# Delta rule: where the third substitution and the second and third merges stand

## The chip, the core and the metric

One core of a Trainium2 chip runs the whole program in one launch. The metric is the device time of that launch in microseconds, as the median of several runs. The text names the engines as the profile does: PE (TensorE: matrix products, transposes; PEld is its weight load), DVE (VectorE), ACT (ScalarE), POOL (GpSimd) and SP (SyncE, which only issues transfers). Each works through its own queue in order; they wait for each other through semaphores. POOL and ACT issue transfers too.

## What is computed

Two layers of a mixer and a mixture of experts, over 256 context and 512 latent tokens. In the mixer, eight heads of softmax attention and eight heads of a gated delta rule, run in both directions, share one input and one output projection. The change concerns the delta rule alone. For each chunk of 64 tokens and each head it needs the inverse of a unit lower triangle, `tmat`:

```python
lower = jnp.where(strict, jnp.einsum("bhnid,bhnjd->bhnij", kb, kc) * decay, 0.0)
tmat = lax.linalg.triangular_solve(lower + eye, jnp.broadcast_to(eye, lower.shape),
                                   left_side=True, lower=True, unit_diagonal=True)
u = jnp.einsum("bhnij,bhnje->bhnie", tmat, vc * bc)
w = jnp.einsum("bhnij,bhnjd->bhnid", tmat, kb * jnp.exp(gcum)[..., None])
...
def step(state, xs):
    v_new = u_i - jnp.einsum("bhid,bhde->bhie", w_i, state)
    o_i = jnp.einsum("bhid,bhde->bhie", qd_i, state) + jnp.einsum("bhij,bhje->bhie", a_i, v_new)
    state = state * jnp.exp(gl_i)[..., None, None] + jnp.einsum("bhid,bhie->bhde", kd_i, v_new)
    return state, o_i
```

The scan over the chunks is serial; there are 12 chunks, context first, and the second direction runs backwards through the context's and then the latents' chunks.

## The kernel before, in words

Tokens stand in six tiles of 128 (two of context, four of latents), two chunks in a tile. A layer goes through these stages: normalization; projections with convolutions, in which the triangles are also built and inverted; the attention's loop, in which attention and the serial delta steps are interleaved; output projection and routing; experts.

*Triangles.* They are worked on in three batches of two tiles, `PAIRS = ((0, 1), (2, 5), (3, 4))`. For a batch, `intra_batch` builds the triangles (`delta_intra`): the two 32 x 32 diagonal blocks of each go to memory (`db`), the block off the diagonal stays in SBUF (`uo`). `delta_subst` inverts the diagonal blocks: it loads the batch as `sB`, one 32 x 32 triangle per partition, and runs 31 pairs of DVE operations, a product into `sT` (L821) and a subtraction from `sY` (L822), each pair on the result of the one before. The result goes to memory (`dy`, L823). `delta_merge` loads it in another layout (`yl`, L834), transposes it on DVE (`yt`, L835), multiplies the blocks on PE (L848, L852, in the PSUM tile `mg`), adds the parts up in `xm` (ACT L840, DVE L856) and stores the inverses to memory (`xad`, L857).

*Where these stand.* The string `ORDER` gives the order of the projection stage, by layer. "c" is a convolution's projection, "n" a plain one, "i", "s" and "m" are `intra_batch`, `delta_subst` and `delta_merge` with the number of the batch. All three substitutions and all three merges stand in it; the third merge is its last item.

*The attention's loop.* For each of the 12 delta steps a pattern (`PAT`) is read letter by letter: "f" advances attention by a quarter of a block of 128 queries and one head, "d" advances the delta step by one part, "a" computes a quarter of a modulation chunk from a 1 MB load (`araw`, issued by POOL) and adds it to `ac` (L264, L266, L279, stored at L280). A delta step reads `xad`, `vk` and `qkd` of its two tiles, loaded one step ahead by SP (`step_load`, L867 to L873). Steps 0 to 3 read the tiles of the first batch, 4 and 5 those of the second, 6 and 7 those of the third. Before the loop, `kv_stacks` loads `vl` and `xl` (POOL, L558, L563) and builds the attention's keys and values; `attn_queries` turns the queries (L586).

*PSUM.* Eight banks are three tiles of tag "a", three of tag "c" and one of tag "s", which is two banks wide. Attention's scores (L601, `sc`) take "s", and so does the merge's `mg`. For each block of queries: scores on PE, row maxima on DVE (L605), exp on ACT (L610), scale, turn, split, values.

*Order.* The program is given to a planner that places the instructions of each engine by the program's order and by its own estimate of when they are ready. `pin` fixes an order by hand where `pins(True)` is set; in the loop it is off (L1619).

## Time and profile before

| | us |
|---|---|
| median of three runs | 2127.5 (2121.08 to 2129.52) |
| the profiled execution, its time | 2123.24 |
| the profiled execution, its span | 2121.4 |
| PE busy in the span | 1758.6 (83%) |
| DVE busy | 1272.5 (60%) |
| ACT busy | 882.0 (42%) |
| POOL busy | 839.4 (40%) |

The profile is of one execution; times in it count from the first instruction. "Busy" is the time in which an engine ran an instruction, and a share of the span is a mean over stages with different limits; hence the views by stretch below. A row of a timeline gives start, duration, engine, line of the kernel, operation, tiles (out<-in), and in brackets how long the engine had been idle and what released it.

### The profile page before, as it was taken

The numbers are of one execution on the slowest core, as the hardware profiler recorded it, in microseconds if no ns is written. First come the engines' busy times: TensorE is split into PE (matmuls) and PEld (weight loads), VectorE is DVE, ScalarE is ACT, GpSimd is POOL, SyncE is SP. The second block draws the span as 40 slices with busy tenths as digits, with TensorE's granted clock in tenths as the row PEclk, the third lists the DMA queues.
The fourth block names the chain that finished last, engine by engine and source line by source line (L and its number), as shares of the span: only waits on it lengthen the run. The fifth ranks groups of instructions, "written<-read, shape, count | busy, mean of one in ns | idle before, by whom it ended". The sixth has DMA issues, their size and how long they took to land. (4 is left out here: it accounts for less than half of the span.)

```text
span 2121.4 us, 34943 instructions
## 1 busy us (share of the span) xinstructions
PE 1758.6 (83%) x13579; PEld 1287.2 (61%) x13579; DVE 1272.5 (60%) x2350; ACT 882.0 (42%) x1513; POOL 839.4 (40%) x915
## 2 busy tenths in 40 slices
PE   6998785678887869999996987844897769999995
PEld 4886775456666745565555876733576555566553
DVE  3468995467672445655555579984677453444443
ACT  3454333446561124444444544423565223444442
POOL 4455663253254323324225467640334632233221
PEclk9998897779997989999997998976999779999997
DMA  8223445986627398889854323365972668887872
GB/s 279 72 70 90 117 137 144 260 250 204 195 56 171 103 359 315 328 319 324 327 180 122 92 73 110 93 182 148 311 204 71 177 266 311 328 312 303 313 262 85
DMA packets 227684, 427.76 MB, mean 202 GB/s; under 512 B 83721, under 2 KB 157181, under 8 KB 202940
## 3 DMA queue, kind: packets, MB, share of 16 engines
q1 hardware_dynamic: 171547, 329.09, 46.1%
q0 software_dynamic: 33536, 72.59, 12.1%
q10 hardware_dynamic: 22432, 23.81, 3.3%
q8 instruction: 109, 1.79, 0.4%
q14 instruction: 60, 0.48, 0.1%
HBM read 386.82 MB, written 84.67 MB: 222 GB/s over the span
## 5 line engine op out<-in xcount | busy, mean ns | idle before, releaser
L1351 PE MATMUL pab<-w,xt 128*128 128x512 f32 x1024 | 465.0, 597 | 0.5 <-ACT xt L1345 0.5
L1351 PEld LDWEIGHTS pab<-w,xt 128*128 128x128 f32 x1024 | 189.3, 192 | 191.2 <-issue 186.3
L1405 POOL DMA_INDIRECT yd<-ey,idx x64 | 118.8, 1856 | 469.8 <-DMA yd<-ey,idx 196.1
L1372 DVE TENSOR_TENSOR gl<-gt,gh 128x256 fp32r<-128x256 f32 x64 | 27.2, 425 | 276.9 <-ACT gh L1371 265.2
L1330 DVE TENSOR_TENSOR w2l<-w,w2h 128x2048 fp32r<-128x2048 f32 x64 | 147.3, 2301 | 43.5 <-ACT w2h L1329 40.8
L1371 ACT ACTIVATE gh<-gt 128x256 fp32r<-128x256 f32 x64 | 24.6, 385 | 349.1 <-PE gt L1367 349.1
L486 POOL TENSOR_TENSOR wlo<-wraw,whi 128x1024 fp32r<-128x1024 f32 (+1 forms) x44 | 111.1, 2530 | 83.5 <-ACT whi L485 83.5
L236 PE MATMUL pn<-whi,hh 128*128 128x256 f32 (+1 forms) x432 | 134.5, 314 | 8.7 <-ACT gev L1541 4.7
L236 PE MATMUL pn<-wlo,hh 128*128 128x256 f32 (+1 forms) x432 | 134.2, 312 | 4.6 <-POOL wlo L486 4.6
L236 PE MATMUL po<-woh,m 128*128 128x512 f32 x320 | 114.4, 434 | 28.1 <-ACT m L1040 15.7
L236 PE MATMUL pn<-whi,hl 128*128 128x256 f32 (+1 forms) x432 | 133.3, 313 | 0.7 <-DVE hl L347 0.6
L236 PE MATMUL pt<-hh,wlo 128*128 128x512 f32 (+1 forms) x352 | 124.8, 354 | 0.0
L236 PE MATMUL pt<-hl,whi 128*128 128x512 f32 (+1 forms) x352 | 123.4, 351 | 0.0
L236 PE MATMUL pt<-hh,whi 128*128 128x512 f32 (+1 forms) x352 | 122.5, 348 | 0.0
L1329 ACT ACTIVATE w2h<-w 128x2048 fp32r<-128x2048 f32 x64 | 121.7, 1902 | 0.0
L1393 PE MATMUL py<-w2h,gh 128*128 128x512 f32 x256 | 108.1, 422 | 4.4 <-DVE ey L1400 4.4
L515 DVE SCALAR_TENSOR_TENSOR dT<-xin,cw,dT 128x772 f32<-128x772 f32 x64 | 82.7, 1295 | 43.9 <-ACT dT L513 42.2
L1345 ACT ACTIVATE xt<-xt 128x512 f32<-128x512 f32 x128 | 69.8, 596 | 85.4 <-PE xt L1344 85.3
L1393 PE MATMUL py<-w2l,gh 128*128 128x512 f32 x256 | 102.1, 399 | 0.0
L1393 PE MATMUL py<-w2h,gl 128*128 128x512 f32 x256 | 101.5, 396 | 0.0
L610 ACT ACTIVATE pp<-sc,mx 128x768 f32<-128x768 f32 (+1 forms) x80 | 65.3, 816 | 83.5 <-DVE mx L605 83.2
L236 PEld LDWEIGHTS pn<-whi,hh 128*128 128x128 f32 x432 | 90.8, 211 | 13.5 <-ACT gev L1541 4.9
(391 smaller groups left out, 4443.9 us busy)
## 6 DMA issues: line engine op xcount, KB each, us to landing
w<-w SPq DMA_DIRECT2D x192, 1024.0 KB, 9.2
araw<-ada_w POOLq DMA_DIRECT2D x40, 1024.0 KB, 9.7
wraw<-w_in SPq DMA_DIRECT2D x40, 512.0 KB, 4.3
lk<-vk SPq DMA_DIRECT2D x48, 256.0 KB, 7.2
lx<-xad SPq DMA_DIRECT2D x40, 256.0 KB, 6.9
araw<-ada_w SPq DMA_DIRECT2D x8, 1024.0 KB, 10.6
wr<-w_out SPq DMA_DIRECT2D x8, 1024.0 KB, 5.1
vk<-vr ACTq DMA_DIRECT2D x16, 384.0 KB
```

The costliest lines, as they stand in the source:

```text
L236: self.nc.tensor.matmul(ps, a(k), b(k), start=(first and n == 0), stop=(last and n == 3 * nk - 1))
L486: getattr(nc, eng).tensor_tensor(lo, raw, hi, op=OP.subtract)
L515: nc.vector.scalar_tensor_tensor(dst, xin[:, tap:tap + 772], cw[:, tap, f:f + 1], dst, op0=OP.mult, op1=OP.add)
L610: self.pin(self.nc.scalar.activation(u.p[:, :u.nk * P], u.ps[:, :u.nk * P], AF.Exp, bias=u.mx, accum_out=u.sm))
L1329: self.pin(nc.scalar.activation(hi, src, AF.Copy))
L1330: self.pin(eng.tensor_tensor(lo, src, hi, op=OP.subtract))
L1345: pin(nc.scalar.activation(xt[:, 4 * q:4 * q + 4, :], ps.rearrange("p (k n) -> p k n", k=4), AF.Copy))
L1351: self.pin(self.nc.tensor.matmul(pa.rearrange("p (a f) -> p a f", a=2), xt[:, k, :], w13[:, :, k, :], start=(k == 0), stop=(k == 7)))
L1371: pin(nc.scalar.activation(gh, p3, AF.Copy))
L1372: pin(nc.vector.tensor_tensor(gl, p3, gh, op=OP.subtract))
L1393: pin(self.nc.tensor.matmul(py[:, n * 512:(n + 1) * 512], a[:, j, :], b[:, c], start=(j + m == 0), stop=(j == 1 and m == 2)))
L1405: self.pin(self.nc.gpsimd.indirect_dma_start(out=yd, out_offset=bass.IndirectOffsetOnAxis(ap=idx, axis=0), in_=y, in_offset=None, bounds_c ...
```

## The change

The third substitution and the second and third merges leave `ORDER` and are done inside the attention's loop, on generators that are advanced between the letters of the pattern: the substitution by one pair of operations per letter in steps 0 and 1, the second merge in step 2 and the third in step 4, each in five parts, before letters 0, 6, 9, 13 and 17. The merge's PSUM tiles are now two of tag "c" in place of one of tag "s". The blocks off the diagonal of the second and third batch go to memory (`ud`) and come back as `ul`. The substitution's triangle and result and the merges' `yl` and `yt` share one buffer there (tag "yl"), `xm` has one. For room, `ac`, `ql` and `lq` go from two buffers to one, `uo` from six to four, and `yt2` shares the buffers of `ot`.

```diff
-UO = 6
+UO = 4
+XM = 1
+MG, MG1, MA = {2: 1, 4: 2}, 2, (0, 6, 9, 13, 17)
...
-ORDER = ("c4 c5 c6 c7 S i0 s0 i1 s1 i2 s2 c0 c1 c2 c3 Q n256 n0 x n512 m0 m1 c8 c10 c11 c9 n2304 m2",
-         "c4 c5 c6 c7 S c0 i0 s0 i1 s1 c9 i2 s2 c1 c2 c3 Q n256 n0 x n512 m0 m1 c8 c10 n2304 c11 m2")
+ORDER = ("c4 c5 c6 c7 S i0 s0 i1 s1 i2 c0 c1 c2 c3 Q n256 n0 x n512 m0 c8 c10 c11 c9 n2304",
+         "c4 c5 c6 c7 S c0 i0 s0 i1 s1 c9 i2 c1 c2 c3 Q n256 n0 x n512 m0 c8 c10 n2304 c11")
...
-        acc = pool.tile([P, UNIT], F32, tag="ac", bufs=2, name="ac")
+        acc = pool.tile([P, UNIT], F32, tag="ac", bufs=1, name="ac")
...
-        x = pool.tile([P, 4, P], F32, tag="ql", bufs=2, name="ql")
+        x = pool.tile([P, 4, P], F32, tag="ql", bufs=1, name="ql")
...
-    def delta_subst(self, b, db, dy, pool):
+    def delta_subst(self, b, db, dy, pool, one=False):
+        nc, pin = self.nc, self.pin
+        if one:
+            both = pool.tile([P, 2 * D], F32, tag="yl", bufs=1, name="sBY")
+            B, Y = [both[:, n * D:(n + 1) * D].rearrange("p (a b) -> p a b", a=32) for n in range(2)]
...
+            pin(nc.vector.tensor_tensor(Y[:, j + 1:32, 0:w], Y[:, j + 1:32, 0:w], T3, op=OP.subtract))
+            yield
         self.q("iy").dma_start(dy.rearrange("h q r c -> (h q) r c"), Y)
+        yield
...
+    def delta_merge(self, tts, dy, us, ud, xad, pool):
+        both = pool.tile([P, 2 * D], F32, tag="yl", bufs=1, name="yl")
+        yl, yt = [both[:, n * D:(n + 1) * D].rearrange("p (d t h i) -> p d t h i", d=2, t=2, h=NH) for n in range(2)]
...
+        if us is None:
+            us = {}
+            for j, tt in enumerate(tts):
+                us[tt] = pool.tile([P, NH, 32], F32, tag="ul%d" % j, bufs=1, name="ul")
+                self.q("ild").dma_start(us[tt], ud[j])
+        yield
+        pin(nc.vector.transpose(yt, yl))
...
-        ps = self.psS("mg")
-        pa, pb = ps[:, :512], ps[:, 512:]
+        pa = self.psC("mga")
...
+        pin(nc.scalar.activation(g, pa, AF.Copy, scale=-1.0))
+        x = []
+        for d in range(2):
+            x.append(pool.tile([P, 2, NH, HD], F32, tag="xm", bufs=XM, name="xm"))
+            for q in range(2):
+                pin(nc.scalar.activation(x[d][:, :, :, 32 * q:32 * q + 32], xb[d], AF.Copy, scale=self.C["quad"][:, q:q + 1]))
+        yield
+        pb = self.psC("mgb")
...
-            a = pool.tile([P, 512], F32, tag="lq", bufs=2, name="lq")
+            a = pool.tile([P, 512], F32, tag="lq", bufs=1, name="lq")
...
-            t = pool.tile([P, 512], F32, tag="yt2", bufs=1, name="yt2")
+            t = pool.tile([P, 512], F32, tag="ot", bufs=2, name="yt2")
...
+        if b > 0:
+            for j, tt in enumerate(PAIRS[b]):
+                self.q("iud").dma_start(ud[b, j], us[tt])
...
-            with self.pool("q2", A) as p2:
+            with self.pool("q2", A) as p2, self.pool("mg2", A) as p3:
                 S, seen = [None], set()
+                subst = self.delta_subst(2, db[2], dy[2], p3, True)
...
-                    for c in PAT[i][s % 3]:
+                    for n, c in enumerate(PAT[i][s % 3]):
+                        if s in MG:
+                            if n == 0:
+                                b = MG[s]
+                                assert next(subst, None) is None
+                                merge = self.delta_merge(PAIRS[b], dy[b], None, ud[b], xad, p3)
+                            if n in MA:
+                                next(merge)
+                        if s < MG1:
+                            next(subst, None)
                         next({"d": step, "f": fill, "a": ada}[c], None)
```

## Rows read from the trace of the kernel before

**Rows 1.** The page: tenths of busy time, VectorE, in 40 slices

```profile
DVE  3468995467672445655555579984677453444443
```

**Rows 2.** Busy time by stretch: stretch, length, busy by engine, PEclk, DMA share, GB/s

```profile
187.00:345.00 158.00, 128.06 (x1498) 115.52 (x1497) 152.66 (x313) 57.05 (x111) 89.78 (x80) 0.89 0.38 111
345.00:378.00 33.00, 5.44 (x265) 4.87 (x265) 7.55 (x16) 8.96 (x17) 8.62 (x10) 0.58 0.71 192
378.00:640.00 262.00, 212.00 (x2807) 157.72 (x2808) 174.15 (x369) 145.19 (x293) 104.99 (x109) 0.89 0.68 197
1301.00:1412.00 111.00, 84.37 (x884) 72.83 (x884) 106.53 (x242) 37.92 (x79) 64.25 (x55) 0.86 0.38 107
1412.00:1471.00 59.00, 14.73 (x547) 11.78 (x548) 29.74 (x60) 17.05 (x28) 10.83 (x11) 0.56 0.60 179
1471.00:1641.00 170.00, 144.92 (x2275) 111.63 (x2273) 124.49 (x258) 101.23 (x189) 57.85 (x64) 0.94 0.69 200
```

**Rows 3.** Timeline of SyncE, layer 0: Y leaves and comes back

```profile
342.94 0.33 SPq L823 DMA_DIRECT2D dy<-sY  x1
345.76 6.26 SPq L834 DMA_DIRECT2D yl<-dy  x4
```

**Rows 4.** Timeline of VectorE, layer 0: the third merge's transpose

```profile
362.34 1.25 DVE L835 STREAM_TRANSPOSE yt<-yl 128x1024 f32<-128x1024 f32 x1 [17.21 <-DMA cr<-conv_w]
```

**Rows 5.** Timeline of TensorE: first scores; last projection and qt, layer 1

```profile
377.88 0.55 PE L601 MATMUL sc<-ka,qs 128*128 128x256 f32 x1 [9.23 <-DVE xm L856]
...
1411.11 0.39 PE L236 MATMUL pt<-hh,wlo 128*128 128x512 f32 x1
...
1424.08 0.42 PE L586 MATMUL qt<-cst,ql 128*128 128x128 f32 x1
...
1469.91 0.76 PE L601 MATMUL sc<-ka,qs 128*128 128x512 f32 x1 [5.39 <-DVE xm L856]
```

**Rows 6.** Sums of L821, of L822, both layers; L821 alone; L821 after 1412

```profile
sum 314.00, DVE 92.35; mean DVE 46.18
...
sum 314.00, DVE 85.70; mean DVE 42.85
...
L821 DVE TENSOR_TENSOR sT<-sB,sY x186: 178/377/2585, 187.1 to 1447.3; 128x31 f32<-128x31 f32 x12, 128x60 f32<-128x60 f32 x12, 128x87 f32<-128x87 f32 x12, 128x112 f32<-128x112 f32 x12
...
1412.00:1450.00 38.00, 7.88 (x18) 0.59 0.73 222
```

**Rows 7.** The merges' pieces: last additions, xm's waits, TensorE in one merge

```profile
L856 DVE SCALAR_TENSOR_TENSOR xm<-mg,cst,xm x12: 737/748/752, 302.4 to 1469.0; 128x512 f32<-128x512 f32 x12
...
  DMA xad<-xm: 25.9, 5
...
363.50:369.00 5.50, 3.21 (x252) 0.66 0.41 136
```

**Rows 8.** Timeline of POOL: the attention's first load, by layer

```profile
344.92 0.95 POOL L558 DMA_DIRECT2D vl<-qd  x1
...
1412.67 1.01 POOL L558 DMA_DIRECT2D vl<-qd  x1 [7.65 <-issue]
```

**Rows 9.** The first 56 us of the loops, columns as in rows 2

```profile
378.00:434.00 56.00, 38.56 (x531) 26.44 (x532) 26.07 (x71) 26.27 (x74) 19.32 (x24) 0.74 0.98 278
...
1471.00:1527.00 56.00, 44.69 (x643) 32.45 (x641) 35.87 (x72) 30.42 (x58) 14.05 (x18) 0.89 0.99 294
```

**Rows 10.** Landing of the ten stores of a modulation chunk (L280)

```profile
DMA to landing us min/median/max: 6.2/8.4/10.7
```

**Rows 11.** Timeline, layer 0: a chunk's last add, the next chunk's first copy

```profile
446.35 0.42 DVE L279 TENSOR_TENSOR ac<-ac,ab 128x256 f32<-128x256 f32 x1
...
450.01 0.38 ACT L264 ACTIVATE ac<-aps 128x256 f32<-128x256 f32 x1
```

**Rows 12.** Timeline, layer 1: a POOL issue beside the substitution

```profile
1440.20 0.74 POOL L228 DMA_DIRECT2D araw<-ada_w  x1 [10.53 <-issue]
...
1440.40 0.38 DVE L821 TENSOR_TENSOR sT<-sB,sY 128x207 f32<-128x207 f32 x1
```

More of the change, by code (lines that the diff above doesn't have):

```diff
@@ L807, in delta_intra @@
         self.q("iud").dma_start(db.rearrange("h q j i -> (q j) h i"), src)
-    def delta_subst(self, b, db, dy, pool):
-        nc = self.nc
-        B = pool.tile([P, 32, 32], F32, tag="sB", bufs=SB, name="sB")
+    def delta_subst(self, b, db, dy, pool, one=False):
[3 more added lines that the diff above has]
+            B, Y = [both[:, n * D:(n + 1) * D].rearrange("p (a b) -> p a b", a=32) for n in range(2)]
+        else:
+            B = pool.tile([P, 32, 32], F32, tag="sB", bufs=SB, name="sB")
+            Y = pool.tile([P, 32, 32], F32, tag="sY", bufs=YB, name="sY")
         self.q("ild").dma_start(B, db.rearrange("h q j i -> (h q) j i"))
-        Y = pool.tile([P, 32, 32], F32, tag="sY", bufs=YB, name="sY")
         nc.gpsimd.memset(Y, 0.0)
@@ L834, in delta_merge @@
                 self.q("ild").dma_start(yl[:, d, t], dy[:, n:n + 4].rearrange("h q r c -> (q r) h c"))
-        nc.vector.transpose(yt, yl)
+        if us is None:
[5 more added lines that the diff above has]
+        pin(nc.vector.transpose(yt, yl))
         xb, xt = (yt[:, 0], yl[:, 1]), (yl[:, 0], yt[:, 1])
-        x = [pool.tile([P, 2, NH, HD], F32, tag="xm", bufs=1, name="xm") for d in range(2)]
-        for d in range(2):
-            for q in range(2):
-                nc.scalar.activation(x[d][:, :, :, 32 * q:32 * q + 32], xb[d], AF.Copy, scale=self.C["quad"][:, q:q + 1])
+        yield
         g = pool.tile([P, 512], F32, tag="mg", bufs=1, name="mg")
-        ps = self.psS("mg")
-        pa, pb = ps[:, :512], ps[:, 512:]
+        pa = self.psC("mga")
         place = [(d, 32 * (2 * c2 + d), 32 * (2 * c2 + 1 - d)) for d in range(2) for c2 in range(2)]
@@ L847, in delta_merge @@
             for d, ra, rb in place:
-                nc.tensor.matmul(pa[rb:rb + 32, c], us[tts[t]][ra:ra + 32, h, :], xt[d][ra:ra + 32, t, h, :], start=True, stop=True, tile_position=(ra, rb))
-        nc.scalar.activation(g, pa, AF.Copy, scale=-1.0)
+                pin(nc.tensor.matmul(pa[rb:rb + 32, c], us[tts[t]][ra:ra + 32, h, :], xt[d][ra:ra + 32, t, h, :], start=True, stop=True, tile_position=(ra, rb)))
+        pin(nc.scalar.activation(g, pa, AF.Copy, scale=-1.0))
[4 more added lines that the diff above has]
+                pin(nc.scalar.activation(x[d][:, :, :, 32 * q:32 * q + 32], xb[d], AF.Copy, scale=self.C["quad"][:, q:q + 1]))
+        yield
+        pb = self.psC("mgb")
         for t, h, c in blocks:
             for d, ra, rb in place:
-                nc.tensor.matmul(pb[ra:ra + 32, c], g[rb:rb + 32, c], xb[d][rb:rb + 32, t, h, :], start=True, stop=True, tile_position=(rb, ra))
+                pin(nc.tensor.matmul(pb[ra:ra + 32, c], g[rb:rb + 32, c], xb[d][rb:rb + 32, t, h, :], start=True, stop=True, tile_position=(rb, ra)))
+        yield
         a, b = tts
@@ L855, in delta_merge @@
             y = x[d][:, :, :, 32 - 32 * d:64 - 32 * d]
-            nc.vector.scalar_tensor_tensor(y, pb.rearrange("p (t h i) -> p t h i", t=2, h=NH), self.C["quad"][:, d:d + 1], y, op0=OP.mult, op1=OP.add)
+            pin(nc.vector.scalar_tensor_tensor(y, pb.rearrange("p (t h i) -> p t h i", t=2, h=NH), self.C["quad"][:, d:d + 1], y, op0=OP.mult, op1=OP.add))
             self.q("ix").dma_start(xad[a:b + 1:b - a, d, :, 0].rearrange("t p f -> p t f"), x[d].rearrange("p t h i -> p t (h i)"))
+        yield
     def step_load(self, s, vk, xad, qkd, need, pool):
@@ L994, in token_rows, with intra_batch @@
         self.q("vk").dma_start(dst.rearrange("t p f -> p t f"), r.rearrange("p t e i -> p t (e i)"))
-    def intra_batch(self, b, us, dT, sc, xad, db, pool):
+    def intra_batch(self, b, us, ud, dT, sc, xad, db, pool):
         kk = [self.delta_kk(tt, 1, dT, pool) for tt in PAIRS[b]]
@@ L1591, in layer @@
                         elif kind == "i":
-                            self.intra_batch(int(arg), us, dT, sc, xad, db[int(arg)], p1)
+                            self.intra_batch(int(arg), us, ud, dT, sc, xad, db[int(arg)], p1)
                         elif kind == "s":
-                            self.delta_subst(int(arg), db[int(arg)], dy[int(arg)], p1)
+                            for _ in self.delta_subst(int(arg), db[int(arg)], dy[int(arg)], p1):
+                                pass
                         elif kind == "m":
-                            self.delta_merge(PAIRS[int(arg)], dy[int(arg)], us, xad, p1)
+                            for _ in self.delta_merge(PAIRS[int(arg)], dy[int(arg)], us, None, xad, p1):
+                                pass
                         elif kind == "x":
```

9 lines of the change are left out of this document (3 added, 6 removed).

## The prediction

> **What bounds the kernel now.** I read the page's slices first: VectorE is at 5 to 7 tenths in the projection and delta stages of both layers and at 3 to 5 in the experts [rows 1]. The change touches only the former, so the next view is the busy time by stretch [rows 2]. Six stretches matter, three in each layer.
>
> In layer 0 the second part of the projections (187 to 345) keeps VectorE busy 152.66 of 158 us, TensorE 128.06: VectorE is the bound there. From 345 to 378 nothing is: VectorE 7.55, TensorE 5.44 of 33 us, clock 0.58, that is mostly the lower of TensorE's two levels (1.2 and 2.4 GHz). From 378 to 640 the attention's loop runs, TensorE 212 of 262, VectorE 174.15, so VectorE is idle 88 us in it. Layer 1 repeats this: 1301 to 1412 VectorE 106.53 of 111, then 59 us with TensorE at 14.73, then the loop, TensorE 144.92 of 170, VectorE 124.49.
>
> What ends the hole? In layer 0 the third substitution's result leaves at 342.94 and comes back as yl from 345.76 [rows 3]; VectorE idles 17.21 us before the transpose of the third merge at 362.34 [rows 4]. The releaser named there is a small load; the transpose reads yl, so what it waited for is the way of Y through memory. The merge's PSUM tile is of the "s" tag, which has one buffer ((8-3-3)//2) and which the scores use too: the first scores start at 377.88, released by the merge's last VectorE operation [rows 5]. In layer 1 the first scores wait for the same at 1469.91, though the last projection matmul began at 1411.11 [rows 5]. So a substitution and its merge stand as a serial chain between two dense stages.
>
> **The change, part by part.** The sum is made against the profiled execution (2123.24 us, span 2121.4); the median shown is 2127.5, 4.3 above it, and I carry the difference over.
>
> *Taken from the projections, layer 0.* A substitution is 62 VectorE operations. All six of them cost 92.35 + 85.70 us, 29.7 each [rows 6]; at the median of the products, 62 x 377 ns = 23.4 us [rows 6]. The second merge adds a transpose and two STT operations of 0.75 [rows 7], some 2.7. So 26 to 32 us leave a stage in which VectorE has 5 us to spare. TensorE's 128.06 us stand behind it, so at most 158 - 128 = 30 come back; chains through ACT and POOL hold some. If only the small share that has no TensorE beside it came back, it would be the 5 us. I take 20, bounds 5 and 30.
>
> *Layer 1.* Of the third substitution's 31 pairs 18 run after 1412 [rows 6], so 13 pairs are in the stage: 13/31 of 29.7 = 12 us at most. I take 6, bounds 0 and 12.
>
> *The hole.* Attention's set-up starts with POOL's load of vl, at 344.92 and 1412.67, behind the projections' last work [rows 8]; from there to the first scores it is 33.0 us in layer 0 and 57.2 in layer 1. What is then left of it is the set-up's own chain. In layer 1 the qt transposes started 11.4 us after vl's issue [rows 5, 8], there behind the second merge's first matmuls; I take 12 us to the first scores, bounds 9 and 19. Gain 21 and 45. The delta chain needs the last value convolution, whose tail in layer 1 (its matmuls end near 1411.5) goes through ACT, VectorE, POOL, a turn and two DMAs; step 0 may be later than attention: -4 us, bounds 0 and -12.
>
> *Substitution in the loop.* One pair per letter of the pattern: steps 0 and the first 4 (layer 0) or 9 (layer 1) letters of step 1. In the first 56 us VectorE is busy 26.07 in layer 0 and 35.87 in layer 1 [rows 9], so some 24 us of loop have about 13 us free in layer 0, and 20 us have 7 in layer 1. 23.4 us of work then delay the row maxima, for which exp and the next scores wait, by 10 and 16; the set-up's idle VectorE can take a part of it if the planner puts it there. I take 8 and 12; bounds 0 (all in idle time) and 29.7 (none) in each.
>
> *Merges in the loop, two per layer.* The two batches of 128 small matmuls kept TensorE busy 3.2 us in the third merge of layer 0 [rows 7]; VectorE has 2.7 us and ACT five copies. "xm" keeps one buffer, so the second direction's copies wait until the first is in memory: ACT waited so 25.9 us in 5 merges, 5.2 each [rows 7]. While it waits, ACT holds exp behind it and one of three "c" PSUM tiles stays taken. I take 5 us a merge, bounds 3.2 (TensorE alone) and 10 (a loaded landing in the loop, [rows 10]): -20. Queues passed: the loads of yl and ul and the store of x now stand among SyncE's step loads; these are a step ahead, so nothing is charged; a blocked one would cost a landing.
>
> *Fewer buffers.* "ac" falls from 2 to 1: the next chunk's first copy must wait until the last chunk is stored. Before, the last add was at 446.35 and the next copy on ACT at 450.01 [rows 11], while a store took 6.2 to 10.7 us to land [rows 10]; a wait of about 5 us there. Of eight such chunk changes I count 1 us each, as the planner may order other work ahead: -8, bounds 0 and -36. "ql", "lq", "ot" and "uo": nothing, since their readers finish a block or a step before the next load is needed; without that cover one landing each.
>
> Sum: 20 + 6 + 21 + 45 = 92 gained; 4 + 8 + 12 + 20 + 8 = 52 paid; **40 us** net. 2123.2 - 40 = 2083.2, against the median 2127.5 - 40 = 2087.5.
>
> A rule against it: while a substitution pair ran, POOL issued a 1 MB load in 0.74 us at 1440.20 beside the VectorE operation of 0.38 us at 1440.40 [rows 12], so neither is stretched. The Trainium skill (SBUF — State Buffer, "SBUF: two separate sides") says that a DMA issued from POOL starves while VectorE holds the port pair that both share, and this change puts substitutions beside just these loads. By that rule each of about ten POOL issues in the first two steps would wait for one operation, some 4 us a layer (estimate from that page), a net of 32 instead of 40; by the row nothing. I go by the row.
>
> **Rivals.**
> - *A, the forecast:* the hole closes, the loop pays about half of it back. 2045 to 2112.
> - *B, the loop takes nearly all back.* In the first 56 us of both loops the DMA engines are at 0.98 and 0.99 of their time (278 and 294 GB/s) [rows 9], in the hole at 0.71 and 0.60 [rows 2]. The change moves about 5 MB a layer (triangle load, Y's store, two rounds of yl, two of x, ul) into the loop, 17 us at that rate, and it takes away the pause in which the first 1 MB loads landed. Against it: the share falls to 0.68 over the whole loop, so much is prefetch. Two layers: 34 us; net 6, or 20 if only 20 of the 34 show: 2108 to 2122.
> - *C, slower.* Place: ACT's queue in the loop. Twelve waits for a landing (8 chunk changes, 4 second directions) each stop exp and so the next scores, as there is one score buffer. With 92 gained and 37 paid otherwise (4 + 8 + 12, and 4 x 3.2 for the merges' matmuls), the change loses once a wait and what follows costs over 55/12 = 4.6 us; a landing of 6.2 to 10.7 [rows 10] would give that: 12 x 8.4 = 101, a loss of 46: 2173. For it: ACT already waited 5.2 for xm; against it: the planner can put other work ahead, and at 450.01 no wait is to be seen.
> - *D, it doesn't do what it says.* The planner orders the instructions by itself (order pins are off there), and may put the substitution's pairs back among the projections. Then the 26 from the stages is lost, and the 20 in the loop too: 2093.5. Against it: the tile's memory must be free first.
>
> **How the numbers follow.** A 0.62, B 0.22, C 0.11, D 0.05. The likeliest is A: 2087.5. The range reaches to 2045 (the hole closed to 9 us and 30 from layer 0's stage make 108 gained; 4 for the late step, 10 for the substitution, 13 for the merges and nothing for "ac" make 27 paid; 2127.5 - 81), and up to 2120 through most of B; C and the end of B are left out, about 2 in 10. 0.5% is 10.6 us, about what a measurement of this kernel can tell from no change: faster than 2116.9 are A, D and half of B, 0.78; within 0.5% the rest of B and little of C, 0.12; slower 0.10.
>
> **What would show it.** Right: the first scores within 10 to 19 us of vl's issue in both layers, no VectorE transpose of the second or third merge before them, vl's issue earlier by 10 to 30 us in layer 0, loops 15 to 35 us longer than 262 and 170. Wrong: ACT rows that wait for "xad<-xm" or "md<-ac" by 5 us and more (C); the loops' first 56 us at a DMA share near 1 for much longer, with TensorE waiting for araw (B); substitution rows before vl's issue that belong to the third batch (D). The prediction fails most easily in the two loop terms, whose rows come from other surroundings.

## The result, and the profile after

The changed kernel takes 2143.9 us (median; 2139.66 to 2145.61), 1.0081 times the kernel before, 95% interval 1.0057 to 1.0104: slower by 0.8%, where 2087.5 was forecast and 2120 was the range's upper end. Its profiled execution took 2145.2 us, span 2143.4 (before 2123.24 and 2121.4), so the traces differ by 22 us where the medians differ by 16. Times within a kernel are read from its trace.

By layer the traces say: layer 0 reaches its last store before the experts at 731.9 in place of 748.2, 16 us earlier. Layer 1 begins its projections 14.8 us earlier, and its last store of that kind is 21.5 us late: 36 us are lost in layer 1 alone. The six stretches of the kernel after answer to [rows 2] (projections, set-up, loop, layer by layer; columns as there):

```profile
182.00:329.00 147.00, 123.39 (x1231) 112.08 (x1230) 125.11 (x247) 53.14 (x105) 86.15 (x78) 0.90 0.42 127
329.00:341.00 12.00, 3.36 (x20) 2.78 (x19) 3.05 (x7) 5.20 (x11) 9.28 (x12) 0.72 0.88 262
341.00:610.00 269.00, 212.55 (x3254) 160.40 (x3254) 186.21 (x425) 141.47 (x293) 91.15 (x102) 0.83 0.68 197
1284.00:1405.00 121.00, 88.02 (x884) 77.01 (x882) 100.87 (x216) 40.67 (x85) 67.50 (x53) 0.76 0.43 127
1405.00:1420.00 15.00, 6.17 (x33) 4.21 (x34) 9.57 (x14) 8.68 (x15) 9.20 (x9) 0.65 0.91 300
1420.00:1680.00 260.00, 172.60 (x2783) 134.47 (x2783) 152.37 (x329) 108.90 (x201) 61.43 (x70) 0.78 0.62 164
```

The holes are closed: 33 and 59 us became 12 and 15. From the first scores to the last delta output layer 0's loop now takes 269 us (240 before, last section; the 262 of [rows 2] run past that output, which stood at 617.8) and layer 1's 260 (170 before), the latter with TensorE at 172.60 us and a clock of 0.78 in place of 0.94. Layer 1's loop is where the time went. The timeline shows the holes' ends (POOL's load vl and the first scores, for [rows 8] and [rows 5]):

```profile
329.20 0.95 POOL L560 DMA_DIRECT2D vl<-qd  x1
341.08 0.58 PE L603 MATMUL sc<-ka,qs 128*128 128x256 f32 x1 [3.01 <-DVE qs L593]
...
1405.03 1.01 POOL L560 DMA_DIRECT2D vl<-qd  x1 [6.96 <-PE pt L238]
...
1419.60 0.80 PE L603 MATMUL sc<-ka,qs 128*128 128x512 f32 x1
```

**Two pieces of work share the loop,** attention and the chain of twelve delta steps, and the later one ends it. Attention's last row maximum in layer 1 moved from 1624.9 to 1601.2; the last delta step's output moved from 1640.2 to 1680.0. So the chain sets the end in layer 1, and it must be read step by step. The mark is `w` (L943; L924 before), one VectorE operation in each of the steps 0 to 10. From w TensorE makes `su`, from which the next state `S` comes, and with that the next step begins. The steps, as differences of the starts of w in the timeline, layer 1:

| kernel | first w | 0-1 | 1-2 | 2-3 | 3-4 | 4-5 | 5-6 | 6-7 | 7-8 | 8-9 | 9-10 | last output |
|---|---|---|---|---|---|---|---|---|---|---|---|---|
| before | 1478.6 | 8.9 | 13.0 | 21.1 | 9.7 | 16.6 | 16.2 | 14.1 | 15.6 | 11.7 | 17.6 | 1640.2 |
| after | 1435.2 | 11.7 | 16.9 | **57.6** | 10.5 | **30.5** | **23.0** | 16.8 | 11.3 | 7.6 | **35.4** | 1680.0 |

The chain begins 43.4 us earlier and takes 76.7 longer to its last w: 36.5 from step 2 to 3, 20.7 from 4 to 6, 17.8 from 9 to 10, 1.7 in the rest; its last output comes 6.5 later still. -43.4 + 76.7 + 6.5 = +39.8. The tail, the output projection and routing behind the loop, then gains some 18 back.

*Steps 2 to 3.* SyncE's queue in layer 1:

```profile
1424.31 0.50 SPq L886 DMA_DIRECT2D lk<-vk  x1
...
1430.49 0.34 SPq L820 DMA_DIRECT2D sBY<-db  x1
...
1488.65 0.33 SPq L830 DMA_DIRECT2D dy<-sBY  x1
1491.27 2.25 SPq L842 DMA_DIRECT2D yl<-dy  x4
```

and SyncE's waits in 1400:1500 (waited in all, times, longest):

```profile
SPq L830 <- DVE sBY L828: 35.5, 1, 35.5
SPq L886 <- DMA vk<-vr: 28.1, 1, 28.1
```

The triangles' load (sBY) stands behind step 0's load, which waited 28.1 us for the value convolutions' store. The substitution's products run from 1438.7 to 1485.4 among the row maxima. Two things hold the merge of batch 1, whose Y had long been in memory, behind it. Its yl and the substitution's sBY have one tag and one buffer; and on SyncE's queue the load of yl stands behind the substitution's store, which waited 35.5 us for the last pair. No run separates the two. TensorE and VectorE meanwhile (from the timeline):

```profile
1463.72 0.68 DVE L943 TENSOR_TENSOR w<-pz,scs 128x512 f32<-128x512 f32 x1
...
1493.93 0.25 PE L858 MATMUL mga<-yl,ul 32*32 32x32 f32 x4 [0.17 <-DMA yl<-dy]
1495.12 0.68 PE L954 MATMUL su<-w,lk 64*64 64x64 f32 x16
...
1521.33 0.68 DVE L943 TENSOR_TENSOR w<-pz,scs 128x512 f32<-128x512 f32 x1
```

Step 2's w is done at 1464.4, its su starts at 1495.12: it stands behind the merge's first matmuls in TensorE's queue, as in the program, where these come before letter 9 of step 2 and su at letter 10. From the start of w to that of su it is 31.4 us; the same distance was 2.1 before and is 1.6 in the run without the pairs (e12, below). TensorE does not stand still in it: it is busy 22.73 us from 1464 to 1495, mostly with attention's matmuls, and 8 of the layer's 32 row maxima (the 9th to the 16th) are done between the two. So attention runs ahead while the chain stands, and ends early; what the chain has lost remains at the end, when nothing is left to fill TensorE with.

*Steps 9 to 10.* By then attention has ended and the delta steps are alone:

```profile
1623.07 0.75 DVE L961 TENSOR_TENSOR S<-su,se 128x256 f32<-128x256 f32 x2 [1.31 <-PE su L954]
...
1647.70 1.22 DVE L1728 SCALAR_TENSOR_TENSOR s<-s,h 128x1024 f32<-128x1024 f32 x1 [23.89 <-DMA h<-norm_ffn_w]
...
1649.32 1.61 PE L920 MATMUL ks<-S,dT 64*64 64x64 f32 x32 [24.16 <-DVE ot L978]
```

An operation of the tail (L1728) stands ahead of delta step 9's output on VectorE and waits 23.89 us for a load of the tail, which SyncE issues at 1631.37 behind other loads. From 1625 to 1650 TensorE is busy 0.84 us and VectorE 2.26.

### The profile page after: what moved, and what is told of

Same layout as the page of the kernel before. It is cut to its first block, busy times and chain, and to the rows that moved or that the text cites. A ratio compares the mean times of both kernels' runs of the same rounds, so it can differ in the third digit from the quotient of the medians.

```text
span 2143.4 us, 35010 instructions
## 1 busy us (share of the span) xinstructions
PE 1773.7 (83%) x13579; PEld 1304.0 (61%) x13579; DVE 1278.1 (60%) x2350; ACT 881.7 (41%) x1513; POOL 841.7 (39%) x915
## 3 DMA queue, kind: packets, MB, share of 16 engines
q0 software_dynamic: 33536, 72.59, 11.9%
## 5 line engine op out<-in xcount | busy, mean ns | idle before, releaser
L238 PE MATMUL po<-woh,m 128*128 128x512 f32 x320 | 108.6, 418 | 13.3 <-DVE m L1069 8.2
L1366 PEld LDWEIGHTS xt<-cst,xe 128*128 128x128 f32 x512 | 67.9, 192 | 50.2 <-issue 29.8
## 6 DMA issues: line engine op xcount, KB each, us to landing
w<-w SPq DMA_DIRECT2D x192, 1024.0 KB, 10.4
wr<-w_out SPq DMA_DIRECT2D x8, 1024.0 KB, 10.5
```

What stands on the lines that cost most here:

```text
L238: self.nc.tensor.matmul(ps, a(k), b(k), start=(first and n == 0), stop=(last and n == 3 * nk - 1))
L1366: pin(nc.tensor.transpose(ps[:, k * P:(k + 1) * P], xe.rearrange("p (q k) -> p k q", k=8)[:, 4 * q + k, :], self.ident))
```

## The experiments

Each time is a median beside runs of the kernel before on the same chip; the ratio is to those runs. Their median lies between 2123.8 and 2128.9, so a few us between two runs of the table are better read from the ratios. "w 2-3" and "w 9-10" are layer 1's steps as above, "max" and "output" the last row maximum and last delta output of layer 1, all from the trace of one execution.

| run | us | ratio (95%) | w 2-3 | w 9-10 | max | output |
|---|---|---|---|---|---|---|
| changed kernel | 2143.9 | 1.0081 (1.0057 to 1.0104) | 57.6 | 35.4 | 1601.2 | 1680.0 |
| e1 layer 0 only | 2125.2 | 0.9997 (0.9979 to 1.0015) | 15.8 | 13.7 | 1614.4 | 1639.1 |
| e2 substitution before | 2136.3 | 1.0051 (1.0033 to 1.0069) | 29.8 | 13.7 | 1623.3 | 1649.6 |
| e3 tail's loads behind | 2133.1 | 1.0029 (1.0011 to 1.0047) | 55.1 | 35.1 | 1603.4 | 1673.5 |
| e4 triangles first | 2126.0 | 1.0005 (0.9985 to 1.0025) | 56.5 | 35.4 | 1580.0 | 1656.6 |
| e5 merge 1 first | 2148.4 | 1.0110 (1.0088 to 1.0133) | 17.0 | 43.5 | 1593.5 | 1679.6 |
| e6 two ac | 2144.6 | 1.0084 (1.0065 to 1.0102) | 53.6 | 29.9 | 1608.6 | 1680.6 |
| e7 two xm | 2145.2 | 1.0090 (1.0070 to 1.0111) | 60.9 | 33.7 | 1606.7 | 1682.5 |
| e8 layer 0, old PSUM | 2117.7 | 0.9970 (0.9955 to 0.9985) | 20.7 | 17.7 | 1617.4 | 1632.3 |
| e9 one piece, layer 1 | 2112.7 | 0.9941 (0.9919 to 0.9963) | 23.0 | 14.8 | 1600.5 | 1627.1 |
| e10 layer 0, third merge's PSUM | 2124.9 | 1.0000 (0.9980 to 1.0019) | 21.2 | 20.5 | 1606.8 | 1664.3 |
| e11 old order, third merge's PSUM | 2149.9 | 1.0120 (1.0091 to 1.0149) | 21.5 | 20.4 | 1623.5 | 1682.5 |
| e12 no pairs | 2111.8 | 0.9923 (0.9897 to 0.9949) | 31.6 | 19.5 | 1614.3 | 1639.3 |
| e13 all of the tail behind | 2130.6 | 1.0017 (1.0001 to 1.0033) | 56.3 | 11.2 | 1593.0 | 1655.4 |
| e14 one piece, both layers | 2153.5 | 1.0133 (1.0107 to 1.0159) | 25.6 | 18.1 | 1643.9 | 1668.1 |
| e15 and merges earlier | 2157.4 | 1.0135 (1.0112 to 1.0159) | 16.7 | 13.7 | 1645.0 | 1670.3 |
| e16 e9 with old PSUM | 2112.9 | 0.9941 (0.9921 to 0.9962) | 23.1 | 19.5 | 1607.3 | 1624.7 |
| e17 layer 0 pure | 2121.1 | 0.9984 (0.9964 to 1.0004) | 19.9 | 17.6 | 1632.0 | 1647.0 |
| e18 e17 with triangles first | 2101.9 | 0.9903 (0.9872 to 0.9935) | 20.1 | 17.6 | 1602.6 | 1617.5 |

**Rival C: ACT waits for landings.**

```diff
-        acc = pool.tile([P, UNIT], F32, tag="ac", bufs=1, name="ac")
+        acc = pool.tile([P, UNIT], F32, tag="ac", bufs=2, name="ac")
```

> The changed kernel with two buffers for ac again and nothing else. Rival C (ACT's waits for ac's stores, 8 chunk changes): in the trace of the changed kernel one such wait is 4.3 us at 1538 and the rows of this line come to 11 us of idle time in layer 0's loop against 6.6 before; if they count, 2143.9 - 8 to 15 = 2129 to 2136. Theory L: the copies' waits lie beside the delta chain's, 2141 to 2145.

> The changed kernel with two buffers for xm in the loop's merges (the substitution's products use mg's tile for that), nothing else. In the changed kernel ACT waited 5.4 to 7.0 us for the first direction's store in each merge of layer 1. Rival C: 4 x 5 to 7 us come back, 2143.9 - 20 to 28 = 2116 to 2124. Theory L: the merge's own tail gets 5 us shorter, and with it delta steps 4 and 6, some 5 to 10 us in all: 2134 to 2139.

The second run gives the loop's `xm` two buffers in the same way. The waits are there, in the size that rival C needed. What ended ACT's idle time before L266 (ac) and L864 (xm) in the changed kernel (us, times), both layers:

```profile
  DMA md<-ac: 21.5, 5
...
  DMA xad<-xm: 23.9, 5
```

That is 4.3 us each for ac. Of the five waits for xm one, of 2.5 us, belongs to the merge left among layer 1's projections; the four in the loops are 5.4 each. C was to decide from 4.6 on. With two ac no row of L266 waits for a store any more; with two xm only the one outside the loops is left:

```profile
  DMA xad<-xm: 2.5, 1
```

and the time is 2144.6 and 2145.2, as before the edit (for the second run both expectations were lower). So C has its waits, but taking either kind away gives no time back. In the traces that is a sum: layer 0's last store before the experts comes 10 and 13 us later than in the changed kernel, and layer 1 is 9 and 10 us shorter. Whether the edit or the planner's order does this is open, and no run removes both kinds at once.

**The price of the pairs.** The run leaves out the 62 operations of each layer; their loads and stores stay:

```diff
         for j in range(31):
+            if one:
+                yield
+                continue
             m, w = 31 - j, j + 1
```

> The changed kernel without the 31 pairs of the third substitution (Y stays the identity: 62 VectorE operations a layer left out, its loads and stores stay). The price of these operations in the loop by itself. Theory L and rival V both expect a large gain, from the forecast's 8 + 12 = 20 it would be 2124; if the pairs are what delays merge and steps, layer 0 gains 15 and layer 1 about 37 + 24: 2143.9 - 50 to 75 = 2069 to 2094.

2111.8, 32 us less than the changed kernel, where the forecast's two terms gave 20 and the other account 50 to 75. In layer 1, from vl to the last output, 229.4 us in place of 275.0; in layer 0 273.9 in place of 281.2, and layer 0's last store before the experts is not earlier (737.4 and 731.9). So the pairs cost layer 1 about 45 us at its last delta output, part of which the tail gives back, and layer 0 nothing that reaches the end. Steps 2 to 3 still take 31.6 with the second merge in them, 10.5 more than before, and 4 to 5 27.0, 10.4 more: a merge costs the chain 10 us, the pairs 57.6 - 31.6 = 26 in the same place, and the hole of step 9 to 10 goes with them (35.4 to 19.5). Attention, from which the prediction took the pairs' time, is not held up by them: its last row maximum is at 1614.3 without the pairs and at 1601.2 with them. The loops of this run:

```profile
343.00:605.00 262.00, 211.12 (x3244) 158.49 (x3243) 161.61 (x356) 137.88 (x287) 92.20 (x99) 0.84 0.68 196
1425.00:1639.00 214.00, 168.47 (x2797) 130.68 (x2795) 131.69 (x266) 108.72 (x201) 60.18 (x68) 0.83 0.62 177
```

**When they start, and how densely they stand.**

```diff
+                next(subst)
                 kx = load(0)
```

> The changed kernel, but the load of the third batch of triangles is issued ahead of step 0's loads, so that on SyncE's queue it no longer stands behind the one that waited 28.1 us in layer 1 for the value convolutions' store. Theory L: the substitution of layer 1 starts 10 to 14 us earlier, and its chain of delta steps ends as much earlier: 2143.9 - 12 = 2132. Rival V (VectorE's time in the loop sets the pace): the substitution takes as much longer, 2140 to 2146. If this load itself waits for the memory that it lands in, the step loads behind it are late: over 2146.

2126.0: 18 us for the place of one load in each layer (and of the first pair, which `next` runs with it), more than the 12 expected. The load's issue in layer 1 moved to 1406.4, the first pair to 1415.6, but the pairs now take 55 us, and steps 2 to 3 still 56.5. In layer 0 the step from 2 to 3, 60.6 us long in the changed kernel, fell to 41.6, and the last store before the experts came 10.5 us earlier (721.4; 721.3 and 721.6 in e9 and e16, which have this edit too), although attention's last maximum was later (592.6 for 583.5). This speaks for the chain, which ends at 610.4 in the changed kernel, setting layer 0's end there too. Next, the same with the pairs of layer 1 in one piece:

```diff
+                for _ in subst if i in (1,) else ():
+                    pass
...
-                        next({"d": step, "f": fill, "a": ada}[c], None)
+                        with tc.issue_after(self.slast) if s == 0 and i in (1,) else ExitStack():
+                            next({"d": step, "f": fill, "a": ada}[c], None)
```

> The kernel with the triangles' load first, and in layer 1 the 31 pairs of the substitution in one piece: every VectorE operation of delta step 0 and of the attention beside it is queued behind the last pair. In the run without that (2126.0) the pairs stretched from 1414 to 1471 among the row maxima, with VectorE at 24.71 and 21.12 of 25 us, and the second merge could only begin behind them. Theory L (the chain of delta steps sets layer 1's end, and the substitution's end sets the second merge, for which steps 2 to 4 wait): pairs 1411 to 1437, attention's first maxima 25 us later, second merge 30 us earlier, last delta step about 25 us earlier: 2126 - 24 = 2102. Rival V (VectorE's total in the loop sets the end, however the pairs are spread): the same 2126 within 4. If attention's late start is the longer: over 2132.

2112.7. The 31 products of layer 1 (count, duration min/median/max, first and last start) in the changed kernel and then in this one:

```profile
L827 DVE TENSOR_TENSOR sT<-sBY x31: 191/357/771, 1438.7 to 1485.4; 128x31 f32<-128x31 f32 x2, 128x60 f32<-128x60 f32 x2, 128x87 f32<-128x87 f32 x2, 128x112 f32<-128x112 f32 x2
```

```profile
L827 DVE TENSOR_TENSOR sT<-sBY x31: 191/358/426, 1412.1 to 1435.1; 128x31 f32<-128x31 f32 x2, 128x60 f32<-128x60 f32 x2, 128x87 f32<-128x87 f32 x2, 128x112 f32<-128x112 f32 x2
```

Operations of the same median length, 47 us spread, 23 in one piece. Attention's first maximum comes 28 us later than in e4 and its last one 20 later, and yet the last delta output 29.5 earlier: the chain sets layer 1's end, not VectorE's total (rival V). Steps 2 to 3 take 23.0, no hole is left, and the time equals that without the pairs (2111.8). It is 10 us over what was expected; attention now ends 27 us before the chain, where it was 77 in e4. Its ratio, 0.9941 (0.9919 to 0.9963), makes this run faster than the kernel before.

Then the same in layer 0 as well (`i in (0, 1)`):

> As the run with the substitution in one piece in layer 1, but in layer 0 too. Layer 0's pairs are spread over some 50 us, its second merge ends at 441, its step 3 comes 60 us after step 2; but attention sets the end there, not the delta chain. Theory L: the pairs in one piece hold attention's first maxima back by about 20 us, and give the delta chain the same: 2112.7 within 8. Rival V (VectorE's total sets it): 2112.7 within 4.

2153.5, 41 us more: both expectations fell. In layer 0 the first maximum comes at 376.8 in place of 343.3, the last at 630.7 in place of 588.8, and the last store before the experts at 759.7 in place of 721.3. Layer 0 has 48 row maxima a loop against 32, and attention had only 14 us to spare there against the chain (588.8 to 602.9): held up by 33 us at its start it takes the end along. That it is attention's length and not something else in this order is argued, not shown. In these runs the same 62 operations are better spread in layer 0 and better in one piece in layer 1.

**Merge 1 ahead of the substitution.** `MG` becomes `{0: 1, 4: 2}`, the pairs follow in steps 1 and 2:

> The changed kernel with the order of two pieces exchanged in both loops: the second merge (whose Y has long been in memory) in step 0, the third substitution after it in steps 1 and 2, one pair a letter as before; the third merge stays in step 4, all buffers as changed. In the changed kernel the second merge's yl shares its 8 KB with the substitution, so it cannot begin before 1491, and delta step 2's su stands behind its matmuls in TensorE's queue: w goes 15 to 21 us a step, but 57.6 from step 2 to step 3. Theory L: steps 2 and 3 of layer 1 take 35 to 40 us in place of 57.6 plus the step before, the chain ends 30 to 40 us earlier, and nothing of it is left to mix with the tail: 2143.9 - 35 = 2109 (2100 to 2118). Rival V (VectorE's 26 us in the loop set it): the wait moves to step 4, whose merge now waits for the substitution: 2140 to 2146.

Theory L's 2109 fell: 2148.4. Steps 2 to 3 do fall to 17.0, but steps 4 to 5 take 56.0: the pairs now run from 1460 to 1529, 70 us, and the third merge, which needs their result, waits for them. The order of the two is not the cause; whichever merge stands behind a substitution that is spread out waits for it.

**The substitution back among the projections,** the merges in the loop (`s2` in `ORDER` again):

> The third substitution goes back among the projections in both layers; the second and third merge stay in the loop, with all buffers as changed. Theory L (in layer 1 the substitution starts late in the loop, and the merges, whose buffer it holds, and the delta steps come late behind it): layer 0 loses the 11 us that its projections had gained, layer 1's chain ends about 40 us earlier, 2143.9 + 11 - 40 = 2115. Rival C (the loss is ACT waiting for landings of ac's and xm's stores, 12 of them, none removed here): about 2144 + 11 - 10 = 2145. Rival V (VectorE has too little time left in the loop for the 26 us, wherever in it they stand): 2144 + 11 - 2 x 15 = 2125.

2136.3, between the theories: in its trace layer 1 loses 5 us in place of 36 (steps 2 to 3 and 4 to 5 are those with a merge, 29.8 and 26.8, and there is no hole), but layer 0's 16 gained become 5 lost, with vl at 340.7 in place of 329.2. The substitution's place in the loop is layer 0's gain and layer 1's loss.

**The hole of step 9.** The tail's modulation loads and their operation are queued behind the last step; in a second run the router's loads, the residual rows and the first gating of o too:

```diff
+                with (tc.issue_after(self.lend) if n == 0 else ExitStack()), (tc.issue_after(self.dend) if n == 0 else ExitStack()):
+                    for nm, ch in (("g2", 2), ("m3", 3), ("s4", 4)):
```

> The changed kernel, but the first modulation loads of the tail (and their VectorE operation, which waited 23.9 us at 1648 ahead of delta step 9) are queued behind the last delta step's loads and its last VectorE operation. Theory L with this hole as its largest piece: 2143.9 - 20 = 2124 (2120 to 2129). Rival: the tail needs these loads anyway and waits for them at its own place, so the hole moves: 2140 to 2146.

> As the run with the tail's modulation loads behind the last delta step, and also the router's loads, the residual rows and the first gating of o (VectorE) behind it. There the hole had moved: step 10's w stood at 1658.35 on VectorE behind the gating's reduction, which waited through ACT and POOL for the landing of a step load that was queued on SyncE behind the tail's loads. If these queues are the whole of the hole: step 10's w about 15 us behind step 9's, last delta step about 1650 in place of 1673: 2133 - 20 = 2113. If the steps stood still for another reason: 2128 to 2138.

2133.1, and the step is still 35.1 long. In that run's timeline the hole had moved:

```profile
1633.57 1.19 SPq L887 DMA_DIRECT2D lx<-xad  x2
...
1651.17 1.26 POOL L892 TENSOR_TENSOR lx<-lx,lq 128x512 f32<-128x512 f32 x1 [20.68 <-DMA lx<-xad]
1652.51 2.59 POOL L985 TENSOR_TENSOR o<-o,ot 64x512 f32<-64x512 f32 x2
1655.13 0.63 ACT L1042 ACTIVATE o<-o 128x512 f32<-128x512 f32 x1 [30.46 <-POOL o L985]
1655.80 0.69 DVE L1044 TENSOR_REDUCE oss<-o 128x8 f32<-128x512 f32 x1 [24.74 <-ACT o L1042]
...
1658.35 0.68 DVE L943 TENSOR_TENSOR w<-pz,scs 128x512 f32<-128x512 f32 x1
```

Read upwards: w stands behind the gating's reduction, that behind ACT, that behind POOL, and POOL behind a step load that SyncE issued late, among loads of the tail. With all of that behind the last step the step takes 11.2 us, and the time is 2130.6, 13 less than the changed kernel. From the run before, in which the hole was still there, that is no clear step (ratios 1.0017 and 1.0029, intervals overlapping), and the expected 2113 was not reached, since the last two outputs now lie 19 us apart (1636.3 and 1655.4):

```profile
1650.95 1.04 POOL L1129 COPY mb<-m3t 128x1024 f32<-128x1024 f32 x1 [19.71 <-DMA m3t<-md]
1651.95 2.59 POOL L985 TENSOR_TENSOR o<-o,ot 64x512 f32<-64x512 f32 x2
1654.57 0.76 DVE L978 TENSOR_TENSOR ot<-pq,scs 128x256 f32<-128x256 f32 x2 [15.79 <-POOL o L985]
```

The last output waits for POOL, which has yet to read step 10's output, behind a copy of the tail. Its buffer is the one that step 10's output still holds: in the changed kernel the tag "ot" has two buffers, and yt2 takes the other one. The prediction had put "ot" at nothing.

**Each layer by itself.**

> Layer 0 as changed, layer 1 in the old order (third substitution, second and third merge among its projections). In the trace of the changed kernel layer 0 reaches its experts 16 us earlier than before and layer 1 then loses 38. Theory L (the loss is layer 1's alone: its chain of delta steps ends long after its attention): 16 us faster than before, 2127.5 - 16 = 2111.5, ratio 0.992. Rival S (both layers pay the same, and layer 0's lead is only prefetch that layer 1 gives back): half of the whole loss, 2127.5 + 8 = 2136, ratio 1.004.

2125.2, neither theory. Layer 0 kept its 16 us up to the experts; layer 1, in the old order, lost 14 of them, as its projections took 31 us longer. There TensorE waited before the merges' first matmuls (busy, mean ns of one, idle time before):

```profile
L858 PE MATMUL mga<-yl,uo 32*32 32x32 f32 x256 | 4.5, 237 | 32.3 <-DMA yl<-dy 21.1 <-DVE yl L849 11.2
```

The merge's PSUM had been changed with the rest, from the one 1024-wide tile to two of the 512-wide ones. Putting that back:

> Layer 0 only, as before, with one more thing set back: merges that stand among the projections use the one 1024-wide PSUM tile again in place of two of the three 512-wide ones. With the latter the planner put both merges of layer 1's projections ahead of the last projections, and TensorE waited 32.3 us for their yl and its transpose (18.1 before): the stage took 31 us longer than before, which ate layer 0's 16. If the PSUM tile is what let them go there: layer 1 back to its old length, 2127.5 - 16 = 2111 (2106 to 2117). If something else did (the shared yl buffer, the extra stores of ud): 2122 to 2130.

2117.7: 7 us of the expected 14 came back (6 by the ratios). Then only the third merge, the one on which the scores wait, on the small tiles, with layer 0 as changed and with layer 0 as before:

> Layer 0 as changed; layer 1 in the old order, the second merge on the 1024-wide PSUM tile, only the third merge on two of the 512-wide ones, so that the scores need not wait for it. With all on the 1024-wide tile (2117.7) the first scores of layer 1 stood at 1451.6, 49 us behind vl. If the PSUM tile is what holds the scores: first scores 12 to 15 us behind vl, a gain of some 35 us of which the delta chain, whose steps start as before, lets 5 to 15 through: 2103 to 2113. If the planner pulls the third merge ahead of the last projections again, as with two merges: 2125 or more.

> Both layers in the old order (nothing in the loop), the smaller buffers as changed, with only the third merge's PSUM moved to the 512-wide tiles. Tells how much of the hole was the PSUM tile and not the place of the work: layer 0's first scores at 345 to 360 in place of 378, and 2127.5 - 10 to 25 = 2102 to 2118 if attention sets the end of layer 0; 2120 to 2130 if the chain of delta steps does, which starts where it did.

2124.9 and 2149.9, so neither gained. The first scores did come earlier: in the first run's layer 1 they stand 25.7 us behind vl (47.2 in e8; the 1451.6 of the expectation is the first row maximum), in the second run's layer 0 at 365.1 in place of 377.9. But in layer 1 of both the tail's operation again stood ahead of the last delta steps, and waited 17 and 19 us. That hole needs neither substitution nor merge in the loop. The second run has nothing in the loop, only the changed buffers and the third merge's PSUM tile, and it is slower than the changed kernel. So a loss of this size does not by itself point to the pairs. What points to them is that the changed kernel's loss goes when they are left out (e12) or stand in one piece in layer 1 (e9). And e9 with the large tile:

> As the run with the substitution in one piece in layer 1, and the first merge, the one left among the projections, back on the 1024-wide PSUM tile in both layers. TensorE waited 14.1 us for its yl and transpose in layer 1 (7.1 before). If the tile lets the planner put it too early: 2112.7 - 5 to 8 = 2105 to 2108. If not: 2110 to 2115.

2112.9, no gain: vl came 9 us earlier (1384.4), the first w 2.5. One step of merges earlier than needed, against e14, is no gain either (2157.4 for 2153.5):

> As the run with one piece in both layers, but with the merges in steps 1 and 3 in place of 2 and 4, one step before the last in which they are in time. If the steps behind a merge wait for its result (x through memory): 5 to 15 us faster than that run. If what a merge costs is its place in TensorE's and ACT's queues, which goes along: the same within 5.

Last, layer 1 with everything of before, its buffers and its merge too:

> Layer 0 as changed; layer 1 with the order, the merge, the PSUM tile and all buffers of before. Theory L (layer 0's 16 us are real, layer 1's part of the change alone loses): 2127.5 - 16 = 2111.5 (2106 to 2116). If layer 1 gives a lead back whatever its code: 2120 to 2128.

> The same with layer 0's triangles loaded ahead of step 0's loads. In the three runs with that, layer 0 left its experts 27 us earlier than before in place of 16. Theory L: 2127.5 - 27 = 2100.5 (2095 to 2106). If that was another placement by chance: as the run without it, 2106 to 2116.

2121.1 and 2101.9. The first is 0.16% under the kernel before, which its interval does not tell from no change; its trace has layer 0 ahead by 11 us and layer 1, with the source of before, 14 us longer (this execution took 2127.9, 7 over the median). The second keeps its whole lead of 24. The traces show one difference in the planner's work: in e18 layer 1's 707 ACT operations stand in the order of the kernel before, one for one; in e17 151 of them stand at another place. **e18 has the lowest median here** and is faster than the kernel before and the changed one: 0.9903 (0.9872 to 0.9935), an interval that overlaps those of e9 and e16. Its loops:

```profile
345.00:607.00 262.00, 213.41 (x3256) 159.58 (x3257) 187.01 (x424) 141.98 (x292) 91.38 (x99) 0.83 0.69 198
1447.00:1617.00 170.00, 144.82 (x2265) 111.30 (x2264) 124.65 (x256) 101.02 (x189) 57.91 (x64) 0.94 0.70 198
```

## Why the prediction was wrong

The sign was wrong. Layer by layer: the sum had layer 0 at 20 + 21 - 8 - 10 - 4 = 19 gained, and the trace shows 16 at the end of its tail. It had layer 1 at 6 + 45 - 4 - 12 - 10 - 4 = 21 gained, and 36 were lost. Of its own signs, the loops 15 to 35 us longer held in layer 0 (29, to the last delta output) and not in layer 1 (90).

- **The holes:** right. Vl to the first scores is 11.9 and 14.6 us, where 12 (9 to 19) stood. But the 45 us of layer 1 were attention's; the chain's first w came 43.4 earlier, only 28.6 more than the 14.8 with which layer 1 began, since step 0's load waits 28.1 for the value convolutions' store. For the chain the sum's 6 + 45 - 4 = 47 were 28.6.
- **Layer 0's projections:** vl came 15.7 earlier, 4.7 of it before the first substitution: 11, inside 5 to 30, for 20.
- **Layer 1's projections:** 6 (0 to 12) became a loss of some 8: the matmuls take 273.5 us from first to last in place of 265.5. TensorE waited 11.2 us for the first merge's yl and transpose (7.1 for yl before), and the clock was 0.76 in place of 0.86. With the large PSUM tile back they take 264.6 (e16, for 273.4 in e9; 271.5 in e8 for 296.7 in e1), so the tile, which the prediction didn't price outside the loop, accounts for it. In e16's time the 9 us did not show.
- **Substitution in the loop, the step that failed.** It was priced as VectorE time taken from attention's row maxima, 12 in layer 1. Attention was not held up (above). The chain of steps sets the end, and for it the spread pairs are latency: 26 us from step 2 to 3 and 45 at the last delta output by the run without pairs, part of it the hole of the tail. In layer 0 the term (8) measured 7 at the last delta step and nothing at the last store. Both terms together, 20 in the sum, are worth 32 us of the time (e12). The hole goes with a chain that is late behind attention: in the eight kernels with an operation of the tail ahead of a delta step the last output lies 57 us or more behind the last row maximum, in those without 27 or less (e13, where the tail is queued behind, 62). That lateness opens it is read from this, not tested.
- **A buffer left out.** The list of fewer buffers named five tags and not "yl", in which the substitution's two tiles and a merge's two share 8 KB. It ties the second merge to the third substitution, as does the order of SyncE's queue; which of them alone would do so is open.
- **Merges, 5 each:** 10.5 and 10.4 in layer 1's chain, just past the bound of 10, again as latency. "Nothing is charged" for the queues passed was wrong too: on SyncE's queue yl's load stood behind a store that waited 35.5 us, and the triangles' load, which the prediction did not count among them, behind a load that waited 28.1; moving this one load with the first pair gave 18 us (e4).
- **ac:** -8 for eight waits of about 1 us each. There are five of 4.3, and no time came back without them (e6).
- **The clock** was not priced at all (below).

Of the rivals, *B* fell: the first 56 us of the loops now have the DMA engines at 0.90 and 0.62, below the 0.98 and 0.99 of [rows 9]:

```profile
341.00:397.00 56.00, 39.24 (x484) 27.71 (x484) 41.02 (x111) 25.72 (x73) 18.14 (x22) 0.71 0.90 251
1420.00:1476.00 56.00, 40.41 (x404) 30.93 (x403) 45.23 (x105) 30.24 (x56) 8.89 (x12) 0.79 0.62 172
```

*C* had the sign and the waits, but the loss did not go with either of them. *D* fell: every pair stands behind vl. The rule of the Trainium skill (SBUF — State Buffer, "SBUF: two separate sides") that was weighed against [rows 12] was taken to have POOL's issues wait for VectorE's substitution. As that section of the Trainium skill has it, the descriptors starve under VectorE operations in a two-port mode, and an operation with two inputs in SBUF, as the substitution's are, holds the shared pair only against GpSimd operations that read SBUF; it does not by itself give the wait that the prediction worked out. The issues of the 40 loads of araw take a median of 745 ns before and after, and the five loads that POOL issued between 1436 and 1462, while the pairs ran, took 0.72 to 0.80 us each: the trace shows no such wait.

What stays open: how much of each run's few us is the planner's order and how much the edit. Layer 1 of e17 and of e18 come from one source and differ by 16 us in their traces, so single differences of that size between runs aren't proof. The readings above rest on steps that repeat: 53.6 to 60.9 from step 2 to 3 in all six kernels that spread the pairs over layer 1's first steps ahead of merge 1, and 15.8 to 31.6 in all others.

## What to carry to other kernels

Where two pieces of work share a loop, find out which of them ends it in each layer, and by how much, and price what is moved in by that one's measure: busy time beside work that is bound by an engine, latency beside a chain of steps. The same 62 operations were better spread in one layer and better in one piece in the other. For every tile of the moved piece ask who must be done with its buffer and what stands behind its load in the queue. After a move, read where the planner has put the next stage's first operations: one that waits for a load can stand ahead of the last work of the stage before.

## What the runs showed of the hardware

In the loops the granted clock fell with the change: before, layer 0's loop by itself reads

```profile
378.00:618.00 240.00, 193.07 (x2730) 142.90 (x2731) 157.07 (x348) 133.40 (x278) 89.37 (x98) 0.89 0.69 201
```

and after 0.83, with TensorE busy 212.55 us. The merges' 512 small matmuls are 2.92 + 2.83 us of the 19.5 more; the rest goes with the lower mean clock, since but 12 matmuls are added beside them. Why the clock is lower in layer 0 is open; it is not the pairs (0.84 without them). In layer 1 0.94 became 0.78. In the stretch from 1625 to 1650, in which TensorE was busy 0.84 of 25 us, the clock was 0.56, and in the 25 us behind it, busy 10.46, 0.50, the lower of the two levels throughout; in e18, whose layer 1 has the old order, the loop is back at 0.94. So in layer 1 the matmuls behind the hole ran slower too, which no sum of durations taken from the trace of before contains.
